# Moving averages in three parts at three places of a tile, and all of memory's weights loaded ahead of the first head

## The chip, the cores and the metric

The kernel runs on one core of a Trainium2 chip. The metric is the device time of one execution in microseconds (us). The core has five engines with an instruction stream each: TensorE (PE in the profile, its weight loads PEld), VectorE (DVE), ScalarE (ACT), GpSimd (POOL) and SyncE (SP), which here only issues DMA transfers. TensorE's results go to PSUM, of which one "bank" holds 128 x 512 numbers in f32.

## The reference

One layer of a hybrid encoder over 2048 rows of 1024 numbers: an attention with forget gates beside a pooling over moving averages, then a cross attention to 256 memory rows, then a SwiGLU network. What the change touches lies in the first projection, the pooling, and the memory's keys and values:

```python
xn = rmsnorm(h, g_mix)
z = einsum('bsd,dc->bsc', xn, w_in)        # q, k, v (512 each), p_in (512), f_logit (8)
q, k = rmsnorm(q heads, g_q_fox), rmsnorm(k heads, g_k_fox)
c = cumsum(log_sigmoid(f_logit))           # along the sequence
fox = softmax(q.k / 8 + c[t] - c[s], s <= t) . v
mixed_g = trailing mean of p_in over POOL_WINDOWS[g] - p_in     # windows 2, 4, 8, 16
pool = concat(mixed_g . w_pool[g]) * pool_scale
h = h + concat(fox, pool) . w_out
...
mkv = rmsnorm(mem, g_mem_kv) . w_mem_kv    # memory's keys and values
```

## The kernel before

**Products.** Operands of f32 are split in two: a rounded high part, which ACT writes as a cast (L199, or L194 where a gain is applied), and the rest, which VectorE writes as a subtraction (L55). A product is three matmuls (`mm3`, L60 to L62): high by high, high by low, low by high. The cast and the subtraction together are called a split; the second needs the first.

**Order.** From L236 to the end of the memory projection the order of PE, VectorE, ACT, POOL and SP is the order in which the code is written. An engine that stands at an instruction whose inputs are late holds up all that is written behind it on that engine.

**The tiles.** After a first part that makes the pooling's columns (p_in) and splits the weights, sixteen projection tiles i of 128 rows follow (15 in a loop, the last written out). A tile is four quarters n; a quarter (`project`) is 24 matmuls of 128 x 386 into one of four banks "z", which ACT empties with a scaling into z (`scaled`). Between the quarters of tile i the code puts:

- after quarters 0 and 1, `to_heads`: PE turns the heads of tile i-2 (transposes, L425) into three banks "tp", ACT copies them out and SP stores them. Their source kl is the split of the normed heads;
- then `po()`: ACT empties the pooling's one bank "ss" (L493) and POOL stores it; then `pooled`, the three matmuls of one average of the tile before into that bank;
- after quarter 2, `window`: the averages of this tile. VectorE scales and sums (L204, g+1 sums for window 2 << g), takes the mean minus the frame (L474), and then the average is split (ACT L199, VectorE L55) into two new slots "jl". Tiles 0, 3, 6 and 9 make two averages, tiles 1, 2, 4, 5, 7, 8, 10 and 11 one, the others none;
- after quarter 3, `split_heads` for tile i-1: two products on VectorE (L411, L413) norm the heads in cb, ACT casts them to kl (L416), VectorE subtracts (L55).

Fourteen slots jl of 128 x 528 are shared by averages, pooling results, weights on the way in and out (`out_sums`, stores of wo_t at L518), and the gates' cumulation; a freed slot is taken again in the order of freeing, and a taker waits for the slot's last readers, stores among them.

**The last tile** runs its quarters in the order 3, 2, 1, 0. Behind quarter 3 stand four small matmuls of the memory's mean squares (L660, into "ss", from a slot jl). `gates` adds a bias to the gates' logits (L384). `cumulated` is a generator whose phases are put between other work by `next(cum)`: POOL makes a triangle (L529); minimum and doubling on VectorE and exponential and logarithm on ACT (L534 to L537); a difference (L539); two products of PE into "ss" and a running total on POOL; the last sum (L549); a turn by PE, a copy (L553) and a store to memory, from which `load_gates` spreads it over 128 partitions (cb).

**The memory projection** follows: `kv(n)`, n = 0 to 15, six matmuls of 128 x 512 each, from weights that SP loads (`load_kv`, L566, raw in kr) and ACT and VectorE split (`split_kv`, L194 and L195, into kw). Six weights come early; the other ten are loaded here, eight ahead of the first head's loads and two behind kv(4), into eight buffers kr, eight buffers kw. `load_head` fetches the first head of the attention in parts n of 512 columns (qs, kh, kl). In the middle stand the norm's sums for the last tile (L394), its `split_heads` (behind kv(4)) and its transposes (behind kv(7)). The attention starts with a mask on POOL (L832, from cb) and its scores on PE (L841).

The loop's order in code, which the change rewrites:

```python
for n in range(4):
    zps.update(project(i, j, hs, ls, (n,)))
    if n < 2 and i > 1:
        to_heads(i - 2, zr, range(2 * n, 2 * n + 2))
    for po in pos:
        po()
    ...
    if n < 3:
        scaled(i, n, z, zps[n])
    if n == 2:
        nxt = [(w, window(...)) for w in averages(i)]
...
if i > 0:
    zr = split_heads(*st_)
```

Of the kernel before, what the change touches and what calls it, by code (L numbers as in the profile page):

```python
# [25 lines left out]
NG = 4  # L26
# [14 lines left out]
def block_kernel(ctx: ExitStack, tc: tile.TileContext, x, xT, memT, cols, rows, w_qkvf, w_p, w_pool, w_out,  # L41
# [194 lines left out]
    with xstack, in_order(EN.DVE, EN.Activation, EN.Pool, EN.SP):  # L236
# [171 lines left out]
        def split_heads(z, qn, rq):  # L408
# [5 lines left out]
                               op=ALU.mult)  # L414
            zr = slab(2, zs_home, F32R)[:].rearrange("p (h a d) -> p h a d", h=2 * H, a=2)
# [33 lines left out]
        def window(g, T, s):  # L449
# [29 lines left out]
            mh, ml = Slot(F32R), Slot(F32R)  # L479
            split(mh.v, ml.v, mixed)  # L480
# [81 lines left out]
        def load_kv(n):  # L562
            a, k = divmod(n, KD)
            s = Slot() if n < EARLY else None
            kvraw[n] = s, s.v if s else kvp.tile([P, MW], F32, tag="kr", name="kr", bufs=8)[:]
            sp.dma_start(kvraw[n][1], w_mem_kv[k * P:(k + 1) * P, a * MW:(a + 1) * MW])  # L566

        def split_kv(n):
# [5 lines left out]
            else:  # L574
                t_ = kvp.tile([P, 2, MW], F32R, tag="kw", name="kw", bufs=8)
# [22 lines left out]
        for b in range(NB):  # L598
            hs, ls = x_parts(xt)
            for j in range(2):  # L600
# [15 lines left out]
                for n in range(4):  # L616
                    zps.update(project(i, j, hs, ls, (n,)))
                    if n < 2 and i > 1:
                        to_heads(i - 2, zr, range(2 * n, 2 * n + 2))
                    for po in pos:  # L620
                        po()
                    pos = []
                    if mxs:
# [4 lines left out]
                    if n == 2:  # L628
                        nxt = [(w, window(w % NG, w // NG, pts.pop(w))) for w in averages(i)]
                mxs = nxt  # L630
                if i < 6:
                    square_rows(i + 10)
                if i > 0:
                    zr = split_heads(*st_)
# [18 lines left out]
        z, vq = slab(i % 2), slab(3)  # L653
        cum = cumulated()
        next(cum)
        zp3 = project(i, 1, hs, ls, (3,))[3]
        ssp = one_bank()
# [17 lines left out]
        scaled(i, 1, z, zp1)  # L675
# [4 lines left out]
        next(cum)  # L680
# [11 lines left out]
        next(cum)  # L692
        split_kv(4)
# [13 lines left out]
        for n in range(EARLY + 8, 2 * KD):  # L707
            load_kv(n)
# [1102 lines left out]
```

## Time and profile before

| | us |
|---|---|
| median of 3 runs | 2616.28 (2612.10 to 2616.97) |
| the profiled execution | 2612.79 |
| its span, first to last instruction | 2610.8 |
| ahead of the tiles, 0 to 102.2 | 102.2 (PE busy 95.1) |
| sixteen tiles, 102.2 to 437.4 | 335.2 |
| memory projection and start of attention, 437.4 to 515 | 77.6 |
| attention, cross attention, network, 515 to 2610.8 | 2095.8 (PE busy 2050.4) |

The durations in the trace come from the one profiled execution. Of the page, one reads first the busy time of each engine, then the chain of work that ended last (PE 47% of it; the next are "issue" with 8% and VectorE with 2%), then where PE is idle and what it waits for. A row of the trace gives start, duration, engine, line, operation, output<-inputs, tile and shape, and in brackets the idle time ahead of it with what ended it. TensorE's clock can be granted at less than full speed; a view by windows gives the mean grant for any stretch (1.00 is full).

### The profile page before, as it was taken

What the parts mean: (1) busy time and instruction counts of PE and PEld (TensorE: products, weight loads), DVE (VectorE), ACT (ScalarE), POOL (GpSimd) and SP (SyncE); (2) the same over time, 40 slices, a digit from 0 to 9 for tenths busy, and PEclk for the clock granted to TensorE, in tenths of its full rate; (3) what the DMA queues carried; (4) which work ended last, traced back from release to release, by engine and by line L of the source; (5) the groups of instructions that cost most, each with busy time, mean ns of one, the idle gap of its engine ahead of it and who ended that gap; (6) DMA issues with size and microseconds to landing.
All of it is one profiled execution on the core that took longest, in us unless ns stands there. A gap on an engine that the chain in (4) does not pass through costs nothing.

```text
span 2610.8 us, 37299 instructions
## 1 busy us (share of the span) xinstructions
PE 2524.1 (97%) x12909; PEld 2162.6 (83%) x12909; DVE 1730.0 (66%) x2998; ACT 1300.5 (50%) x2487; POOL 825.8 (32%) x1135
## 2 busy tenths in 40 slices
PE   8999898899999899999999999999999999999998
PEld 8989898688888677788878888888888888888887
DVE  4465654799999755454787788656766666664554
ACT  5544344688989622555643433334553333333443
POOL 0022333455545521444524454441001122222000
PEclk9999999999999999999999999999999999999999
DMA  8655565754542645322554554447773233334765
GB/s 278 206 158 157 156 194 176 232 145 124 140 129 62 193 145 180 131 81 94 176 211 154 191 180 174 173 162 244 260 256 139 93 125 105 115 107 165 242 208 187
DMA packets 246765, 434.00 MB, mean 166 GB/s; under 512 B 30000, under 2 KB 119856, under 8 KB 238896
## 3 DMA queue, kind: packets, MB, share of 16 engines
q1 hardware_dynamic: 213104, 322.54, 39.1%
q0 software_dynamic: 33472, 109.08, 11.6%
q8 instruction: 102, 1.67, 0.3%
q14 instruction: 87, 0.71, 0.1%
HBM read 294.02 MB, written 137.50 MB: 165 GB/s over the span
## 4 chain that ended last, share of the span: by engine, by line
PE 47%; issue 8%; DVE 2%; ACT 1%; DMA 1%; POOL 1%; SPq 0%; POOLq 0%; DVEq 0%; ACTq 0%
PE bk L60 13%; PE bk L62 13%; PE bk L61 13%; PE mmps L60 2%; PE mmps L62 2%; PE mmps L61 2%; PE tp L1022 1%; DMA xraw<-hTd 0%; DVE ww L55 0%; POOL out_dram L1704 0%; DMA h<-h1d 0%; ACT mq L1195 0%; DMA hTd<-hst 0%; DVE ms L1199 0%; ACT pm L1224 0%
## 5 line engine op out<-in xcount | busy, mean ns | idle before, releaser
L55 DVE TENSOR_TENSOR ww<-draw,ww 128x512 fp32r<-128x512 f32 x308 | 205.1, 702 | 156.5 <-ACT ww L199 156.0
L199 ACT CAST ww<-draw 128x512 fp32r<-128x512 f32 x308 | 179.6, 620 | 220.4 <-PE bk L62 173.3
L55 DVE TENSOR_TENSOR ww<-graw,ww 128x512 fp32r<-128x512 f32 x220 | 177.6, 814 | 106.5 <-ACT ww L199 106.2
L61 PE MATMUL bk<-ww,ww 128*128 128x512 f32 x616 | 239.6, 389 | 0.0
L60 PE MATMUL bk<-ww,ww 128*128 128x512 f32 x616 | 239.6, 389 | 0.0
L62 PE MATMUL bk<-ww,ww 128*128 128x512 f32 x616 | 239.6, 389 | 0.0
L199 ACT CAST ww<-graw 128x512 fp32r<-128x512 f32 x220 | 135.9, 622 | 181.2 <-PE bk L62 159.5
L55 DVE TENSOR_TENSOR pl<-tp,ph 128x512 fp32r<-128x512 f32 (+3 forms) x296 | 176.9, 599 | 32.4 <-ACT ph L935 30.5
L60 PE MATMUL zps<-wh,xhi 128*128 128x386 f32 x512 | 176.6, 345 | 0.0
L854 ACT ACTIVATE s<-s,mx 128x1024 f32<-128x1024 f32 (+2 forms) x192 | 173.7, 905 | 4.7 <-DVE mx L848 4.2
L62 PE MATMUL zps<-wh,xl 128*128 128x386 f32 x512 | 175.0, 342 | 0.0
L61 PE MATMUL zps<-wl,xhi 128*128 128x386 f32 x512 | 174.9, 342 | 0.0
L919 PE MATMUL tp<-ident,s 128*128 128x128 f32 x1088 | 171.8, 273 | 3.1 <-DVE pl L55 2.5
L935 ACT CAST ph<-tp 128x512 fp32r<-128x512 f32 (+3 forms) x296 | 148.8, 514 | 39.8 <-PE tp L919 34.0
L919 PEld LDWEIGHTS tp<-ident,s 128*128 128x128 f32 x1088 | 133.9, 141 | 31.6 <-DVE pl L55 6.7
L1704 POOL DMA_DIRECT2D out_dram<-o x32 | 17.3, 542 | 382.5 <-DVE o L1701 381.5
L62 PE MATMUL bk<-qs,ww 128*128 128x512 f32 x352 | 137.2, 390 | 1.1 <-DVE ww L55 1.1
L60 PE MATMUL bk<-qs,ww 128*128 128x512 f32 x352 | 137.8, 392 | 0.3 <-ACT s L1623 0.3
L61 PE MATMUL bk<-kh,ww 128*128 128x512 f32 x352 | 137.0, 389 | 0.0
L60 PE MATMUL bk<-kl,ww 128*128 128x512 f32 x352 | 136.9, 389 | 0.0
L61 PE MATMUL bk<-cb,ww 128*128 128x512 f32 x352 | 136.9, 389 | 0.0
L62 PE MATMUL bk<-kl,ww 128*128 128x512 f32 x352 | 136.9, 389 | 0.0
(612 smaller groups left out, 7276.8 us busy)
## 6 DMA issues: line engine op xcount, KB each, us to landing
graw<-in_w_gu_dram SPq DMA_DIRECT2D x44, 1024.0 KB, 5.4
draw<-in_w_down_dram SPq DMA_DIRECT2D x66, 256.0 KB, 4.5
xl<-in_xT_dram SPq DMA_DIRECT2D x64, 256.0 KB, 4.4
wdr<-in_w_down_dram SPq DMA_DIRECT2D x22, 512.0 KB, 4.6
jl<-in_x_dram SPq DMA_DIRECT2D x32, 256.0 KB, 6.9
vd<-cb SPq DMA_DIRECT2D x16, 512.0 KB, 3.7
cb<-cd SPq DMA_DIRECT2D x8, 1024.0 KB, 7.2
v<-vd SPq DMA_DIRECT2D x8, 1024.0 KB, 5.1
```

The source lines that it names most:

```text
L55: (eng or dve).tensor_tensor(out=lo, in0=src, in1=f(hi), op=ALU.subtract)
L60: pe.matmul(ps, lhsT=sh, rhs=mh, start=first, stop=False, skip_group_check=goes_on)
L61: pe.matmul(ps, lhsT=sh, rhs=ml, start=False, stop=False, skip_group_check=goes_on)
L62: pe.matmul(ps, lhsT=sl, rhs=mh, start=False, stop=last, skip_group_check=goes_on)
L199: act.copy(hi, raw)
L854: act.activation(s[:, sl], s[:, sl], AF.Exp, bias=ng, scale=-1.0, accum_out=l[:, q, g:g + 1])
L919: pe.transpose(tp[:, q * P:(q + 1) * P], unit["rows"][q][:, j * P:(j + 1) * P], ident[:])
L935: act.copy(ph[:, sl], tp[:, sl])
L1022: pe.transpose(tp[:, e_], src[:, q + e_], ident[:])
L1704: pool.dma_start(out[rows_, cs], o)
```

## The change

The tile loop: `split_heads` loses its two products to a new `norm_heads`; `window` ends with the mean, and its split becomes `window_cast` (ACT) and `window_rest` (VectorE). The averages' sums now stand behind quarter 0, their casts behind quarter 1, followed by the norm products of tile i-1 and the averages' subtractions; `split_heads` (cast and subtraction) comes right behind quarter 3. `po()` moves ahead of `to_heads`.

The last tile: the memory's mean squares move behind quarter 2, the heads' norms and split ahead of the cumulation's second phase, the cumulation's products behind quarter 1, its last sum behind kv(1).

The memory projection: ten buffers kr and seven kw; ten loads in one go; the gates' load between parts 1 and 2 of the first head; the last tile's transposes behind kv(8).

```diff
-        def split_heads(z, qn, rq):
+        def norm_heads(z, qn, rq):
             qf = qn.rearrange("p (h d) -> p h d", d=DH)
...
+        def split_heads(z, qn, rq):
+            qf = qn.rearrange("p (h d) -> p h d", d=DH)
             zr = slab(2, zs_home, F32R)[:].rearrange("p (h a d) -> p h a d", h=2 * H, a=2)
             act.copy(zr[:, :, 0, :], qf)
...
-            mh, ml = Slot(F32R), Slot(F32R)
-            split(mh.v, ml.v, mixed)
+            return s
+
+        def window_cast(s):
+            mh = Slot(F32R)
+            act.copy(mh.v, s.t[:, HIS:])
+            return s, mh
+
+        def window_rest(s, mh):
+            ml = Slot(F32R)
+            sub_hi(ml.v, s.t[:, HIS:], mh.v)
             s.free()
             return mh, ml
...
-            kvraw[n] = s, s.v if s else kvp.tile([P, MW], F32, tag="kr", name="kr", bufs=8)[:]
+            kvraw[n] = s, s.v if s else kvp.tile([P, MW], F32, tag="kr", name="kr", bufs=10)[:]
...
-                t_ = kvp.tile([P, 2, MW], F32R, tag="kw", name="kw", bufs=8)
+                t_ = kvp.tile([P, 2, MW], F32R, tag="kw", name="kw", bufs=7)
...
-                    if n < 2 and i > 1:
-                        to_heads(i - 2, zr, range(2 * n, 2 * n + 2))
                     for po in pos:
                         po()
                     pos = []
+                    if n < 2 and i > 1:
+                        to_heads(i - 2, zr, range(2 * n, 2 * n + 2))
...
-                    if n == 2:
-                        nxt = [(w, window(w % NG, w // NG, pts.pop(w))) for w in averages(i)]
+                    if n == 0:
+                        wins = [(w, window(w % NG, w // NG, pts.pop(w))) for w in averages(i)]
+                    if n == 1:
+                        wins = [(w, window_cast(s_)) for w, s_ in wins]
+                        if i > 0:
+                            norm_heads(*st_)
+                        nxt = [(w, window_rest(*s_)) for w, s_ in wins]
                 mxs = nxt
+                if i > 0:
+                    zr = split_heads(*st_)
                 if i < 6:
                     square_rows(i + 10)
-                if i > 0:
-                    zr = split_heads(*st_)
...
         zp3 = project(i, 1, hs, ls, (3,))[3]
+        scaled(i, 3, z, zp3)
+        gates(i, z)
+        norm_heads(*st_)
+        zr = split_heads(*st_)
+        next(cum)
+        zp2 = project(i, 1, hs, ls, (2,))[2]
         ssp = one_bank()
...
-        scaled(i, 3, z, zp3)
-        gates(i, z)
         next(cum)
-        zr = split_heads(*st_)
...
-        zp2 = project(i, 1, hs, ls, (2,))[2]
-        next(cum)
-        next(cum)
...
         zp1 = project(i, 1, hs, ls, (1,))[1]
+        next(cum)
...
         to_heads(i - 1, zr, range(4))
-        next(cum)
...
         kv(1)
         next(cum)
+        next(cum)
...
-        for n in range(EARLY, EARLY + 8):
+        for n in range(EARLY, 2 * KD):
             load_kv(n)
-        head0.extend(load_head(0, hpa, range(3)))
+        head0.extend(load_head(0, hpa, range(2)))
         load_gates(0, head0[3])
+        load_head_part(0, head0, 2)
...
         split_kv(7)
-        for n in range(EARLY + 8, 2 * KD):
-            load_kv(n)
+        norm_heads(*st_)
         zr = split_heads(*st_)
...
-        to_heads(LAST, zr, range(4), pool)
         split_kv(10)
         kv(8)
+        to_heads(LAST, zr, range(4), pool)
```

The order of instructions at three places. First VectorE in tile 3, from the mean of the first average to the split of the heads (jl are slots of averages, cb the normed heads, kl their split). Before:

```order
L474 SCALAR_TENSOR_TENSOR jl_1796<-jl_2129,jl_1796 128x512
L55 TENSOR_TENSOR jl_2133<-jl_1796,jl_2132 128x512
L204 TENSOR_TENSOR jl_1798<-jl_1798,jl_1794 128x512
L457 COPY jl_1798<-tail_1428 128x16
L459 COPY tail_1428<-jl_1798 128x16
L204 TENSOR_TENSOR jl_2139<-jl_1798 128x527
L204 TENSOR_TENSOR jl_2141<-jl_2139 128x525
L474 SCALAR_TENSOR_TENSOR jl_1798<-jl_2141,jl_1798 128x512
L55 TENSOR_TENSOR jl_2145<-jl_1798,jl_2144 128x512
L411 TENSOR_TENSOR cb<-qs,zrq 128x1024
L413 TENSOR_TENSOR cb<-cb,gqs 128x1024
L55 TENSOR_TENSOR kl<-cb,kl 128x16x64
```

and after, VectorE at the same place:

```order
L477 SCALAR_TENSOR_TENSOR jl_1796<-jl_2059,jl_1796 128x512
L204 TENSOR_TENSOR jl_1798<-jl_1798,jl_1794 128x512
L460 COPY jl_1798<-tail_1428 128x16
L462 COPY tail_1428<-jl_1798 128x16
L204 TENSOR_TENSOR jl_2065<-jl_1798 128x527
L204 TENSOR_TENSOR jl_2067<-jl_2065 128x525
L477 SCALAR_TENSOR_TENSOR jl_1798<-jl_2067,jl_1798 128x512
L411 TENSOR_TENSOR cb<-qs,zrq 128x1024
L413 TENSOR_TENSOR cb<-cb,gqs 128x1024
L55 TENSOR_TENSOR jl_2120<-jl_1796,jl_2114 128x512
L55 TENSOR_TENSOR jl_2122<-jl_1798,jl_2116 128x512
L55 TENSOR_TENSOR kl<-cb,kl 128x16x64
```

The two subtractions L55 of the averages, which stood each behind its own average, now stand together behind both averages and behind the two norm products.

Second, VectorE in the last tile, from the gates' bias (L384) to the turned sums (jl is here the slot of the cumulation, mms the memory's mean squares). Before:

```order
L384 TENSOR_TENSOR fl<-kh,rowt 128x8
L534 TENSOR_SCALAR jl_4432<-fl 128x128
L535 SCALAR_TENSOR_TENSOR jl_4432<-jl_4432,fl 128x128
L411 TENSOR_TENSOR cb<-qs,zrq 128x1024
L413 TENSOR_TENSOR cb<-cb,gqs 128x1024
L55 TENSOR_TENSOR kl<-cb,kl 128x16x64
L667 COPY mms<-ss 128x2
L539 TENSOR_TENSOR jl_4432<-jl_4432 128x128
L545 COPY jl_4432<-ss 128x128
```

and after, VectorE between the same two ends:

```order
L384 TENSOR_TENSOR fl<-kh,rowt 128x8
L411 TENSOR_TENSOR cb<-qs,zrq 128x1024
L413 TENSOR_TENSOR cb<-cb,gqs 128x1024
L55 TENSOR_TENSOR kl<-cb,kl 128x16x64
L545 TENSOR_SCALAR jl_4430<-fl 128x128
L546 SCALAR_TENSOR_TENSOR jl_4430<-jl_4430,fl 128x128
L550 TENSOR_TENSOR jl_4430<-jl_4430 128x128
L686 COPY mms<-ss 128x2
L55 TENSOR_TENSOR cb<-kh,cb 128x8x64
L556 COPY jl_4430<-ss 128x128
```

The heads' three instructions moved ahead of the gates' first two, and the split of the values (cb<-kh,cb) ahead of the copy of the cumulation's products from "ss".

Third, VectorE in the memory projection at the cumulation's last sum, which is L549 before and L560 after (kw are split weights, zms the sums of squares of the last tile's heads). Before:

```order
L195 SCALAR_TENSOR_TENSOR jl_4558<-jl_4024,colt,jl_4557 128x512
L195 SCALAR_TENSOR_TENSOR jl_4562<-jl_4026,colt,jl_4561 128x512
L549 TENSOR_TENSOR jl_4432<-ss,jl_4433 128x128
L195 SCALAR_TENSOR_TENSOR kw<-jl_4028,colt,kw 128x512
L195 SCALAR_TENSOR_TENSOR kw<-jl_4204,colt,kw 128x512
L394 TENSOR_REDUCE zms<-cb 128x16
L553 COPY jl_4432<-ss 128x128
```

and after, VectorE in the same stretch:

```order
L195 SCALAR_TENSOR_TENSOR jl_4558<-jl_4024,colt,jl_4557 128x512
L195 SCALAR_TENSOR_TENSOR jl_4562<-jl_4026,colt,jl_4561 128x512
L195 SCALAR_TENSOR_TENSOR kw<-jl_4028,colt,kw 128x512
L195 SCALAR_TENSOR_TENSOR kw<-jl_4204,colt,kw 128x512
L394 TENSOR_REDUCE zms<-cb 128x16
L560 TENSOR_TENSOR jl_4430<-ss,jl_4431 128x128
L564 COPY jl_4430<-ss 128x128
```

The last sum moved behind two weights' splits and the reduction, right ahead of the copy of its own turn.

More of the change, by code (lines that the diff above doesn't have):

```diff
@@ L652, in block_kernel @@
         i = LAST
-        z, vq = slab(i % 2), slab(3)
         cum = cumulated()
         next(cum)
+        z, vq = slab(i % 2), slab(3)
         zp3 = project(i, 1, hs, ls, (3,))[3]
+        scaled(i, 3, z, zp3)
[4 more added lines that the diff above has]
+        zp2 = project(i, 1, hs, ls, (2,))[2]
         ssp = one_bank()
```

## The prediction

> **What bounds the kernel now.** I read the page first, then the stages in windows, then the waits of TensorE in the stage that the change touches, and last the single waits in order of time.
>
> ```profile
> span 2610.8 us, 37299 instructions
> PE 2524.1 (97%) x12909; PEld 2162.6 (83%) x12909; DVE 1730.0 (66%) x2998; ACT 1300.5 (50%) x2487; POOL 825.8 (32%) x1135
> 102.20:437.40 335.20, 314.73 (x1825) 308.15 (x1824) 195.90 (x299) 152.46 (x267) 98.56 (x103) 0.97 0.56 164
> 437.40:515.00 77.60, 63.90 (x309) 46.87 (x308) 51.05 (x135) 49.42 (x97) 29.98 (x54) 0.96 0.78 230
> ```
>
> TensorE is busy 97% of the span, so only time in which it stands or runs at a lower granted clock can be won. The windows' columns are length, then busy time of PE, PEld, DVE, ACT and POOL, then granted clock, share of the DMA engines and GB/s. The sixteen projection tiles (102 to 437 us) leave PE 20.5 us idle at a clock of 0.97; the memory projection and the start of attention behind it leave 13.7 us at 0.96. VectorE is busy for 196 of 335 us there: it is late in places, not overloaded. The waits of PE from 102 to 515 us by group (sum, times, longest), the first and the last of the four long ones in the tiles, and those of the memory projection:
>
> ```profile
> PE tp L425 <- DVE kl L55: 15.3, 6, 3.1
> PE ss L60 <- ACT jl L493: 4.3, 3, 1.4
> 184.06 1.21 PE L425 MATMUL tp<-identr,kl 128*128 128x128 f32 x8 [2.93 <-DVE kl L55]
> 317.12 1.20 PE L425 MATMUL tp<-identr,kl 128*128 128x128 f32 x8 [2.85 <-DVE kl L55]
> 420.40 1.83 PE L660 MATMUL ss<-ones,jl 128*128 128x1 f32 x8 [3.44 <-POOL jl L529]
> 455.00 1.18 PE L425 MATMUL tp<-identr,kl 128*128 128x128 f32 x12 [2.73 <-DVE kl L55]
> 471.93 0.80 PE L60 MATMUL kv<-kw,xhi 128*128 128x512 f32 x1 [4.36 <-ACT kw L194]
> ```
>
> Six times the transposes wait for the split of the normed heads (kl); the wait before 455.00 is one of them, the other five lie in tiles 3, 4, 7, 9 and 10 and make 15.3 - 2.73 = 12.6 us. Three times, in tiles 4, 7 and 10, the second pooling matmul waits for ACT to empty its one bank: 4.3 us. Together 16.9 us. The last three rows belong to the last tile and the memory projection.
>
> **The clock behind a wait.** The granted clock is the last but two of each row.
>
> ```profile
> 184.10:187.50 3.40, 3.40 (x15) 3.11 (x16) 2.58 (x4) 3.01 (x5) 0.49 (x1) 0.51 0.37 101
> 317.20:320.60 3.40, 3.40 (x15) 3.11 (x16) 3.30 (x8) 2.97 (x5) 2.14 (x4) 0.51 0.38 121
> 455.10:458.50 3.40, 3.39 (x25) 2.90 (x26) 1.33 (x3) 2.95 (x6) 2.07 (x3) 1.00 1.05 210
> 419.60:426.50 6.90, 6.10 (x22) 6.13 (x23) 5.68 (x11) 3.07 (x5) 0.96 (x3) 0.51 0.14 40
> 470.80:477.70 6.90, 5.78 (x13) 4.23 (x14) 3.27 (x5) 3.28 (x5) 1.88 (x4) 0.51 1.05 253
> ```
>
> Behind the first and the last of the four long waits in the tiles follow 3.4 us at half clock; behind the waits of 3.44 and 4.36 us nearly seven; behind that of 2.73 us none. Four stretches cost at most 4 x 3.4 x 0.49 = 6.7 us; I take 6.0 (1.5 each), since short transposes fill part of them. The two long ones cost 0.49 x 6.1 = 3.0 and 0.49 x 5.8 = 2.8 us. [...]
>
> **The tiles.** VectorE's chain in tile 3, from the first moving average to the split heads:
>
> ```profile
> 167.56 1.10 DVE L204 TENSOR_TENSOR jl<-jl,jl 128x512 f32<-128x512 f32 x1
> 169.59 0.69 DVE L474 SCALAR_TENSOR_TENSOR jl<-jl,jl 128x512 f32<-128x512 f32 x1
> 173.79 0.69 DVE L55 TENSOR_TENSOR jl<-jl,jl 128x512 fp32r<-128x512 f32 x1 [3.50 <-ACT jl L199]
> 174.40 1.07 DVE L204 TENSOR_TENSOR jl<-jl,jl 128x512 f32<-128x512 f32 x1
> 177.15 0.69 DVE L474 SCALAR_TENSOR_TENSOR jl<-jl,jl 128x512 f32<-128x512 f32 x1
> 179.18 1.22 DVE L411 TENSOR_TENSOR cb<-qs,zrq 128x1024 f32<-128x1024 f32 x1
> 182.77 1.23 DVE L55 TENSOR_TENSOR kl<-cb,kl 128x1024 fp32r<-128x1024 f32 x1 [1.11 <-ACT kl L416]
> ```
>
> VectorE starts the averages at 167.56 with nothing else to do, yet stands 3.5 us for ACT's cast, which waits behind the third scaling. With the sums together, both are done 3.44 us (174.40 to 177.84) after 170.28, at 173.7; the two norm products take it to 176.2, the two subtractions to 177.5, ACT's head cast (about 1.1 us) lies beside these, and the split ends near 178.8 instead of 184.0. PE wants it at 181.13: the wait goes, with some 2 us to spare. Tiles 4, 7, 9 and 10 have the same order, and 1.4 us waits go because the bank's reading now stands ahead of the head copies on ACT. Nothing is added: the same instructions run. **A: 16.9 + 6.0 = 22.9 us.** What is late next is PE itself.
>
> In later tiles an average also waits for a store that still reads its slot:
>
> ```profile
> 286.06 0.69 DVE L204 TENSOR_TENSOR jl<-jl 128x513 f32<-128x513 f32 x1 [9.06 <-DMA poolT<-jl]
> 270.69 2.14 POOL L518 DMA_DIRECT2D wo_t<-jl  x4 [10.36 <-DVE jl L204]
> ```
>
> With the slots taken in another order, the first sum of that tile needs the first of the four wo_t stores issued at 270.69; their landing has a median of 2.3 us, so it waits little where the old one waited 9.06. I price this at nothing: PE has slack there. At worst it brings half of A back.
>
> **The last tile and the memory projection.** Moving the four sums of squares (L660) behind the next projection takes away 3.44 us and its 3.0 of clock; the data, ready at 420.4, precede their new place at 421. The weights that PE waits for at 471.93 were asked for last:
>
> ```profile
> 445.05 3.70 SPq L566 DMA_DIRECT2D kr<-in_w_mem_kv_dram  x8
> 463.42 0.85 SPq L566 DMA_DIRECT2D kr<-in_w_mem_kv_dram  x2
> 471.15 0.72 ACT L194 ACTIVATE kw<-kr,colt 128x512 fp32r<-128x512 f32 x1 [8.91 <-DMA kr<-in_w_mem_kv_dram]
> 470.40 1.11 POOL L832 TENSOR_SCALAR_AFFINE_SELECT cm<-cb 128x128 f32<-128x128 f32 x3 [4.33 <-DMA cb<-cd]
> 477.57 0.34 PE L841 MATMUL sps<-kh,qs 128*128 128x256 f32 x1
> 460.00:470.00 10.00, 6.93 (x31) 4.57 (x29) 4.55 (x7) 2.25 (x4) 3.31 (x4) 1.00 1.02 325
> ```
>
> In one go, the last two leave some 17 us earlier: 4.36 + 2.8 us go. The DMA engines are full (1.02), so two loads ahead push the first head's parts back by about 2 us, but the gates (cb) move ahead of the third part. They arrived at 470.40 and should now land near 467, and PE, at the first scores at 477.57 before, reaches them near 471, so this cover holds, barely. The transposes of 455.00 come one weight later (1.4 us), and with the chain ahead of them earlier by about as much their 2.73 us go. Removed: 3.44 + 3.0 + 4.36 + 2.8 + 2.73 = 16.3 us.
>
> The change also **adds two waits** of PE. The gates' cumulation now follows the split of the heads:
>
> ```profile
> 421.06 0.23 DVE L534 TENSOR_SCALAR jl<-fl 128x128 f32<-128x128 f32 x1
> 421.65 0.31 ACT L536 ACTIVATE jl<-jl 128x128 f32<-128x128 f32 x1 [2.02 <-DVE jl L535]
> 423.27 0.40 ACT L537 ACTIVATE jl<-jl,ones 128x128 f32<-128x128 f32 x1
> 421.53 1.22 DVE L411 TENSOR_TENSOR cb<-qs,zrq 128x1024 f32<-128x1024 f32 x1
> 425.12 1.22 DVE L55 TENSOR_TENSOR kl<-cb,kl 128x1024 fp32r<-128x1024 f32 x1 [1.11 <-ACT kl L416]
> 443.19 1.21 DVE L394 TENSOR_REDUCE zms<-cb 128x16 f32<-128x1024 f32 x1
> 428.75 0.42 PE L60 MATMUL zps<-wh,xhi 128*128 128x386 f32 x1
> 437.29 1.67 PE L425 MATMUL tp<-identr,kl 128*128 128x128 f32 x16
> ```
>
> From 421.06 run first the heads (421.53 to 426.34: 4.8 us), then minimum and doubling (0.6), then exponential to logarithm (421.65 to 423.67: 2.0) and a difference (0.3): ready at 428.8. PE does two quarters of a tile in 8.5 us (428.75 to 437.29); no longer held from 416.96 (420.40 less 3.44), it has two more quarters and the sums of squares behind it by about 426.4: a wait of 2.5 us (first). Its totals then go through POOL, and the last sum stands behind the reduction of row 443.19. That reduction ends 7.1 us after PE's transposes of row 437.29 start; these now start near 435.1, so the sum is there at 442.5, while PE, in order, has done two weights (1.4 us each, six matmuls apart) by 439.4: 3.1 us (second). The trace of before has neither; the ends are 0, if VectorE runs ahead, and twice 4.36 + 2.8 = 14.3 us, if both become like the longest wait here. With 1.5 us of clock each I take 2.5 + 3.1 + 3.0 = 8.6 us, nearest to the four like waits, and 0.9 us more for small waits of the weights that PE now catches up with. **B: 16.3 - 9.5 = 6.8 us.**
>
> Seven weight buffers instead of eight (kw) cost nothing: the weight that reuses the first is split after four others have been used.
>
> **Sum.** 22.9 + 6.8 = 29.7 us. The profiled execution took 2612.79 us (span 2610.8 and 2.0 around it), which gives 2583.1. The median of the three runs is 2616.28, 3.5 above it; on that footing I predict 2586.6 us.
>
> **Rivals.**
> - *Half of A stays*: the averages wait for stores in the late tiles (as at 286.06) now at the head of a tile, and norms and split stand behind them in VectorE's order. For: 9 us waits exist. Against: the slots' last stores are older. 2586.6 + 11.5 = 2598.
> - *B comes to nothing*: the loads land no sooner as the engines are full, the gates hold up the first scores. For: share 1.02. Against: the order of the loads. 2593.4.
> - *The two added waits don't come* because VectorE and ACT arrive earlier than I reckon: 2586.6 - 8.6 = 2578.
> - *No clock is won*: the 6.0 us stay, for PE cools at other places instead, and the added waits lose none: 2586.6 + 6.0 - 3.0 = 2589.6. Against: the rows of 184.10 and 317.20. [...]
> - *Nothing is won*: VectorE's split stays as late, for the sums of the next tile push it: within 5 us of before, 2613.
> - *Slower*: ACT's cast of the averages now stands in the second quarter of a tile, and behind it the copies of turned heads (three banks) and the scalings (four banks). If the sums are late by more than about 13 us (three quarters of a tile at 4.3 us), PE finds no bank. To end 5 us above before, some 35 us must be lost: 3 us in each of the twelve tiles that hold averages, so sums 16 us late in all of them. 2622. The longest wait of a sum is 9.2 us, against it.
>
> **How the numbers follow.** Forecast 0.47; half of A stays 0.12; B nothing 0.15; no added waits 0.13; no clock won 0.06; nothing won 0.04; slower 0.03. The range from 2576 to 2601 holds the first five with some 2 to 3 us for the spread of the runs (2612.1 to 2616.97), and both ends of the added waits (2578 to 2592.3). Faster by over 0.2% (5.2 us, about what a measurement of this kernel can tell from no change) 0.93; within it 0.04; slower 0.03.
>
> **What would show it.** In the profile after, PE should have no wait of over 1 us for kl in tiles 3 to 10, none for the bank, and the granted clock of the projection stage should rise from 0.97 to about 0.99. PE should wait for VectorE at the cumulation's first product and at its turn. ACT should not wait for kr at the end of the memory projection, and the first scores should start near 448 us, some 30 us earlier than 477.57. Wrong I am if the transposes still wait, if POOL's first select waits for cb beyond PE's arrival, or if what is won by the first scores is lost before the end.

## The result, and the profile after

The changed kernel takes 2581.15 us (median of 4 runs, 2578.56 to 2587.50) against 2614.86 us (4 runs, 2612.10 to 2616.97): 33.7 us less, a ratio of 0.9875 with a 95% interval of 0.9854 to 0.9896. The prediction was 2586.6 us, between 2576 and 2601.

The page of the changed kernel, its span and the busy times of the engines:

```profile
span 2576.9 us, 37301 instructions
PE 2510.7 (97%) x12909; PEld 2154.4 (84%) x12909; DVE 1734.8 (67%) x2998; ACT 1299.4 (50%) x2487; POOL 822.0 (32%) x1135
```

The same instructions run in 33.9 us less. PE's busy time is shorter too (2510.7 after 2524.1 us), although its matmuls are the same 12909: some of them no longer run at half clock (the mean granted clock of the tiles was 0.97 and is 1.00). The stages of the changed kernel in windows (length, busy time of PE, PEld, DVE, ACT, POOL, granted clock, share of the DMA engines, GB/s): the sixteen tiles, then the memory projection up to the first scores.

```profile
102.20:409.10 306.90, 304.25 (x1825) 300.53 (x1824) 195.85 (x298) 152.24 (x267) 93.81 (x96) 1.00 0.61 180
409.10:444.10 35.00, 29.62 (x139) 22.59 (x138) 18.71 (x26) 19.39 (x32) 12.58 (x21) 0.95 0.81 238
```

The tiles took 335.2 us with PE idle for 20.5 and a clock of 0.97. They now take 306.9 us with PE idle for 2.7 and a clock of 1.00; of the 2.7 us, 2.47 are one of the two waits that the change adds, at the end of this stretch. The tiles' problem is gone; what is left stands in the groups of PE's waits from 102 to 490 us (sum, times, longest), the first five:

```profile
PE sps L858 <- DVE mx L860: 6.0, 4, 4.2
PE ss L563 <- DVE jl L560: 2.8, 1, 2.8
PE ss L554 <- DVE mms L686: 2.5, 1, 2.5
PE kv L61 <- DVE kw L195: 1.3, 3, 0.8
PE kv L60 <- ACT kw L194: 1.3, 2, 0.9
```

No group for kl and none for ACT's reading of the pooling's bank is among them. The second and third are the two added waits at the cumulation. The first is at the start of the attention, and one wait of 4.2 us in it was not foreseen.

**Where the time went.** The same matmul can be found in both traces; the difference of its two times, each from its span's start, is the lead of the changed kernel there. It is 24.5 us at the start of the last tile, 33.5 at the first scores, 30.0 after the first 120 us of attention, and 33.9 at the end. So 24.5 us came from the tiles, 9.0 from the last tile and the memory projection, 3.5 were given back at the start of the attention, and 3.9 came behind it, where nothing was changed. The table of leads below shows that the last piece is spread between executions, and that a second execution of the same kernel gave back 1.1 us at the start of the attention and not 3.5.

**The tiles.** VectorE's waits from 102 to 440 us, two groups of the kernel before:

```profile
DVE jl L55 <- ACT jl L199: 44.8, 17, 8.7
...
DVE jl L204 <- DMA poolT<-jl: 14.7, 2, 9.1
```

and the group of the changed kernel that answers to the first:

```profile
DVE jl L55 <- ACT jl L486: 6.1, 5, 1.7
```

VectorE stood 44.8 us for the averages' casts and now stands 6.1; the 14.7 us for stores that still read a slot are gone. Its wait for the cast of the heads (kl) grew from 30.1 to 47.7 us instead, but PE waits for none of it: here the idle time of VectorE cost something only where it made PE late. Tile 3 in time, VectorE and PE of the changed kernel:

```profile
163.71 1.07 DVE L204 TENSOR_TENSOR jl<-jl,jl 128x512 f32<-128x512 f32 x1
...
169.71 1.22 DVE L411 TENSOR_TENSOR cb<-qs,zrq 128x1024 f32<-128x1024 f32 x1
...
173.40 1.23 DVE L55 TENSOR_TENSOR kl<-cb,kl 128x1024 fp32r<-128x1024 f32 x1
...
180.15 0.80 PE L428 MATMUL tp<-identr,kl 128*128 128x128 f32 x8
```

The split of the heads ends at 174.6 us (173.40 + 1.23), 5.5 us before PE turns them; it used to end at 184.0 us, 2.9 us after PE wanted it. The chain also starts earlier, at 163.71 instead of 167.56, since each tile hands less lateness to the next (with the parts at their old place, in the kernel "parts late" below, it starts at 162.30). In the kernel before, VectorE went from the last subtraction to the norm products at 179.18 without a pause, and ACT's cast of the heads waited for them:

```profile
181.70 1.04 ACT L416 CAST kl<-cb 128x1024 fp32r<-128x1024 f32 x1 [1.92 <-DVE cb L413]
```

So in this tile the later place of the norm products and of the heads' split in the code held nothing up; the averages' chain ahead of them did.

**From the last tile to the attention.** The changed kernel in order of time:

```profile
404.27 0.38 PE L554 MATMUL ss<-jl,ones 128*128 128x128 f32 x1 [2.47 <-DVE mms L686]
...
416.43 0.47 PE L563 MATMUL ss<-ident,jl 128*128 128x128 f32 x1 [2.84 <-DVE jl L560]
...
442.67 1.12 POOL L849 TENSOR_SCALAR_AFFINE_SELECT cm<-cb 128x128 f32<-128x128 f32 x3 [2.74 <-DMA cb<-cd]
...
444.07 0.28 PE L858 MATMUL sps<-kh,qs 128*128 128x256 f32 x1
...
458.12 0.69 DVE L860 CUSTOM_DVE_ANT_0 s<-sps,cb 128x512 f32<-128x512 f32 x1 [4.08 <-DMA mkvd<-mkv]
...
458.87 0.80 PE L858 MATMUL sps<-kh,qs 128*128 128x512 f32 x1 [4.18 <-DVE mx L860]
```

The gates (cb) land 1.4 us ahead of the first scores. Then VectorE stands 4.08 us until the projection's results (mkv) are stored: its score rows s take their memory. PE finds no free bank for scores and stands too. Before, no wait of this group was longer than 1.2 us:

```profile
PE sps L841 <- DVE mx L843: 3.0, 4, 1.2
```

### The profile page after: what moved, and what is told of

It is laid out like the page before. It is cut to its first block, busy times and chain, and to the rows that moved or that the text cites. A ratio compares the mean times of both kernels' runs of the same rounds, so it can differ in the third digit from the quotient of the medians.

```text
span 2576.9 us, 37301 instructions
## 1 busy us (share of the span) xinstructions
PE 2510.7 (97%) x12909; PEld 2154.4 (84%) x12909; DVE 1734.8 (67%) x2998; ACT 1299.4 (50%) x2487; POOL 822.0 (32%) x1135
## 3 DMA queue, kind: packets, MB, share of 16 engines
q8 instruction: 102, 1.67, 0.3%
## 4 chain that ended last, share of the span: by engine, by line
PE 49%; issue 8%; DVE 2%; ACT 1%; DMA 1%; POOL 1%; SPq 0%; POOLq 0%; DVEq 0%; ACTq 0%
PE bk L62 13%; PE bk L60 13%; PE bk L61 13%; PE mmps L60 2%; PE mmps L62 2%; PE mmps L61 2%; PE tp L1039 1%; DVE ww L55 0%; PE obk L60 0%; PE obk L61 0%; PE obk L62 0%; DMA xraw<-hTd 0%; POOL out_dram L1721 0%; DMA wqr<-in_w_mem_q_dram 0%; DMA h<-h1d 0%
## 5 line engine op out<-in xcount | busy, mean ns | idle before, releaser
L55 DVE TENSOR_TENSOR ww<-draw,ww 128x512 fp32r<-128x512 f32 x308 | 205.2, 702 | 155.6 <-ACT ww L199 155.1
L55 DVE TENSOR_TENSOR ww<-graw,ww 128x512 fp32r<-128x512 f32 x220 | 177.8, 815 | 105.9 <-ACT ww L199 105.5
L55 DVE TENSOR_TENSOR pl<-tp,ph 128x512 fp32r<-128x512 f32 (+3 forms) x296 | 176.7, 599 | 27.8 <-ACT ph L952 26.0
L60 PE MATMUL zps<-wh,xhi 128*128 128x386 f32 x512 | 174.6, 341 | 0.0
L952 ACT CAST ph<-tp 128x512 fp32r<-128x512 f32 (+3 forms) x296 | 148.7, 514 | 38.3 <-PE tp L936 32.8
```

The source lines that it names most:

```text
L55: (eng or dve).tensor_tensor(out=lo, in0=src, in1=f(hi), op=ALU.subtract)
L60: pe.matmul(ps, lhsT=sh, rhs=mh, start=first, stop=False, skip_group_check=goes_on)
L952: act.copy(ph[:, sl], tp[:, sl])
```

## The experiments

Each changes the kernel before or the changed kernel in one respect. The lead is that over the profile of the kernel before, at the same matmuls (102, 408, 477.6 and 600 us of before, and the end). At 102 us, where the tiles start, nothing has been changed yet: what stands there, up to 1.4 us, is spread between executions, and is taken off where the text speaks of a lead from the tiles' start.

| kernel | tiles' start | last tile | first scores | 600 us | end | median us |
|---|---|---|---|---|---|---|
| changed | -0.1 | 24.5 | 33.5 | 30.0 | 33.9 | 2581.15 |
| changed, again | 0.0 | 24.7 | 33.8 | 32.6 | 30.7 | 2582.93 |
| tiles alone | 0.7 | 25.4 | 24.6 | 23.8 | 19.6 | 2590.89 |
| memory alone | 1.4 | 0.9 | 9.7 | 7.3 | 6.3 | 2609.22 |
| loads 8 and 2 | 0.9 | 25.6 | 28.2 | 27.3 | 26.9 | 2587.01 |
| parts late | 0.9 | 25.5 | 33.0 | 29.8 | 29.3 | 2583.79 |
| one go early | 0.1 | 14.4 | 22.1 | 19.8 | 14.4 | 2594.36 |
| bank read late | 0.7 | 20.5 | 27.7 | 24.5 | 25.5 | 2586.54 |
| rows elsewhere | 1.0 | 25.6 | 33.3 | 28.4 | 26.8 | 2585.07 |
| cumulation early | 1.1 | 25.8 | 37.5 | 35.9 | 33.7 | 2578.53 |
| the same, again | 1.3 | 25.9 | 37.6 | 36.8 | 37.0 | 2578.71 |
| second head later | 0.3 | 24.9 | 32.7 | 30.2 | 29.8 | 2583.89 |
| later and early | 0.2 | 24.8 | 37.4 | 35.9 | 34.7 | 2579.97 |

From the tiles' start, the lead at the last tile is 24.6 or 24.7 us in all ten rows of the table that have the new tile loop whole or with its parts late. What the tile loop wins therefore repeats almost exactly.

### Each half alone

The first kernel takes the new tile loop into the kernel before, the second the new last tile and memory projection:

```diff
 # tiles alone: last tile as before
+        norm_heads(*st_)
         zr = split_heads(*st_)
...
 # memory alone: tile loop as before
                     if n == 2:
                         nxt = [(w, window(w % NG, w // NG, pts.pop(w))) for w in averages(i)]
```

> The kernel before with the change of the tile loop alone; last tile and memory projection stay as they were. Theory (the two halves add up): PE is 24.5 us earlier at the start of the last tile, as in the changed kernel, the waits of 3.44, 2.73 and 4.36 us behind it stay, and the time is 2614.9 - 24.5 = about 2590 us. Rival (the tiles' gain needs the memory loads, because PE then runs ahead of weights asked for late): the waits of the memory projection grow by 5 us or more and the time is 2595 us or above.

> The kernel before with the change of the last tile and the memory projection alone; the tile loop stays as it was. Theory: the five long waits for kl and the three for the bank stay, the first scores start about 9 us earlier than 477.57, about 3.5 us of it are given back at the start of the attention, and the time is about 2609 us (2606 to 2610). Rival (the memory part is worth nothing): 2613 to 2616 us.

2590.89 us (ratio 0.9910, 0.9889 to 0.9931) and 2609.22 us (0.9985, 0.9974 to 0.9997): both theories hold. PE's waits with the tiles alone, three groups:

```profile
PE kv L60 <- ACT kw L194: 6.4, 2, 5.7
...
PE ss L676 <- POOL jl L540: 3.4, 1, 3.4
PE tp L428 <- DVE kl L55: 2.8, 1, 2.8
```

The three waits behind the tiles stay, the one for the late weights 1.3 us longer. In the table the halves add up at the first scores, 24.6 + 9.7 = 34.3 against 33.5; from the tiles' start they are 23.9 + 8.3 = 32.2 against 33.7, so they add up to within 1.5 us. The memory part alone is worth 8 to 10 us at the first scores but only some 5 in the median.

### What in the tile does it

Three kernels undo one part each of the new tile loop. In the first all three parts stand behind the third quarter, where the averages were before; in the second each average is made in one go behind the first quarter; in the third the bank is read behind the transposes again:

```diff
 # parts late
-                    if n == 0:
+                    if n == 2:
                         wins = [(w, window(w % NG, w // NG, pts.pop(w))) for w in averages(i)]
-                    if n == 1:
+                    if n == 2:
                         wins = [(w, window_cast(s_)) for w, s_ in wins]
...
 # one go early
                     if n == 0:
-                        wins = [(w, window(w % NG, w // NG, pts.pop(w))) for w in averages(i)]
-                    if n == 1:
-                        wins = [(w, window_cast(s_)) for w, s_ in wins]
-                        if i > 0:
-                            norm_heads(*st_)
-                        nxt = [(w, window_rest(*s_)) for w, s_ in wins]
+                        nxt = [(w, window_rest(*window_cast(window(w % NG, w // NG, pts.pop(w))))) for w in averages(i)]
+                    if n == 1 and i > 0:
+                        norm_heads(*st_)
 # bank read late
-                    for po in pos:
-                        po()
-                    pos = []
                     if n < 2 and i > 1:
                         to_heads(i - 2, zr, range(2 * n, 2 * n + 2))
+                    for po in pos:
+                        po()
+                    pos = []
```

> The changed kernel with all three parts and the norm products behind the third quarter, where the averages stood before. Theory A (sums of both averages ahead of their casts are enough): the split of the heads ends about 2 us before PE wants it, no wait for kl over 1 us in tiles 3 to 10, 2581 us. Theory B (the earlier place is what matters): waits for kl of 1 to 3 us come back in tiles 3, 4, 7, 9 and 10 and the time is 2588 us or above.

> The changed kernel, but each average is made in one go (sums, cast, subtraction) behind the first quarter. Theory A (the earlier place is enough): no wait for kl over 1 us in tiles 3 to 10, PE at the start of the last tile within 1 us of the changed kernel, 2581 us. Theory B (the three parts are what matters): the waits come back at least in tiles 3 and 9, which make two averages, 2 to 3 us each with 1.7 us of half clock, 2586 us or above.

> The changed kernel with the bank's reading behind the transposes and their copies again. Theory: the three waits for the bank in tiles 4, 7 and 10 come back, 1.4 us each, no half clock behind them, and PE is 4.3 us later at the start of the last tile; 2585 us. Rival (ACT was late because of the averages' casts, which now stand elsewhere): waits under 0.5 us, 2581 us.

**Parts late:** a lead of 25.5 us at the last tile (24.6 from the tiles' start), 2583.79 us, and no group for kl: theory A. The sums of both averages ahead of their casts, with the norm products between casts and subtractions, are enough; the early place is not needed. VectorE still stands 21.4 us for the averages' casts and 18.2 us for stores that read a slot, up to 8.0 us at a time, and PE loses nothing by it.

**One go early:** theory A was right about kl, for which PE no longer waits, and wrong about the time, 2594.36 us. So the early place alone takes these waits away as well, if with less to spare: in tile 3 the split of the heads ends 2.8 us before PE turns them, not 5.5. Another wait came in tile 1. The kernel with one go early, ACT and PE:

```profile
133.90 0.62 ACT L486 CAST jl<-jl 128x512 fp32r<-128x512 f32 x1 [6.43 <-DVE jl L480]
134.43 0.68 ACT L504 ACTIVATE jl<-ss,colt 128x512 f32<-128x512 f32 x1
...
135.16 0.80 PE L60 MATMUL ss<-jl,jl 128*128 128x512 f32 x1 [6.68 <-ACT jl L504]
```

ACT stands 6.43 us at the cast of sums that VectorE has not made yet; behind it on ACT stands the reading of the pooling's bank, for which PE waits. With 1.4 us more at 253 us and 6.8 us of half clock that begin within the long wait, the lead falls from 24.5 to 14.4 us. That is close to the mechanism of the prediction's slower rival (a cast of late sums holds up the emptying of banks on ACT), in one tile instead of twelve. So the cast may stand apart from its sums (changed kernel) or both late (parts late), but not with them in the first quarter.

**Bank read late:** the three waits come back, 1.42 us each, with no half clock behind them: the theory. From the tiles' start the lead at the last tile is 4.9 us smaller (19.8 against 24.7); PE loses 1.62 us at each of the three, 0.20 more than the wait itself. So the new order of the bank's reading is worth its 4.3 us and a little more by itself. One of the three on PE, and on ACT ahead of it the two copies of turned heads and then the bank:

```profile
185.41 1.07 ACT L430 COPY st<-tp 128x512 f32<-128x512 f32 x2 [4.06 <-PE tp L428]
186.37 0.70 ACT L504 ACTIVATE jl<-ss,colt 128x512 f32<-128x512 f32 x1
```

```profile
187.13 0.49 PE L60 MATMUL ss<-jl,jl 128*128 128x512 f32 x1 [1.42 <-ACT jl L504]
```

### The memory's loads and the cumulation

The first kernel asks for two of the ten weights late again; the second moves the gates' phases back ahead of the heads' norms, and the last sum ahead of the third weight's split:

```diff
 # loads 8 and 2
-        for n in range(EARLY, 2 * KD):
+        for n in range(EARLY, EARLY + 8):
             load_kv(n)
...
         split_kv(7)
+        for n in range(EARLY + 8, 2 * KD):
+            load_kv(n)
 # cumulation early
         gates(i, z)
-        norm_heads(*st_)
-        zr = split_heads(*st_)
         next(cum)
...
+        norm_heads(*st_)
         next(cum)
         dve.tensor_copy(mms[:], ssp[:, :2])
         rsqrt(mr[:], mms[:])
+        zr = split_heads(*st_)
...
         to_heads(i - 1, zr, range(4))
+        next(cum)
...
         kv(1)
         next(cum)
-        next(cum)
```

> The changed kernel, but two of the ten weights are again asked for behind the fourth projected weight. Theory (the order of asking counts): PE waits about 4.4 us for the fifteenth weight with up to 2.8 us of half clock, the first scores start 4 to 7 us later than 444.1, and the time is 2584 to 2588 us. Rival (the DMA engines are full, so only their sum counts): no wait over 1.5 us there, 2581 us.

> The changed kernel with the gates' second phase ahead of the heads' norms again, and the last sum ahead of the third weight's split. Theory: the waits of 2.47 and 2.84 us at the cumulation's first product and turn go, with 1.7 us of half clock behind the second; the first scores start about 437 us and the time is about 2574 us. Rival (the full DMA engines set the start of the attention): the first scores are earlier, but the wait of 4.18 us near 458.9 grows by as much, and the time stays at 2580 to 2582 us.

**Loads 8 and 2:** 2587.01 us, as the theory said, with a wait of 2.81 us instead of its 4.4. The kernel with two late loads, ACT and PE:

```profile
444.00 0.72 ACT L194 ACTIVATE kw<-kr,colt 128x512 fp32r<-128x512 f32 x1 [7.43 <-DMA kr<-in_w_mem_kv_dram]
...
444.77 0.79 PE L60 MATMUL kv<-kw,xhi 128*128 128x512 f32 x1 [2.81 <-ACT kw L194]
```

The order of asking counts, though the DMA engines are full (share 0.98 to 1.03 from 424 to 444 us of the changed kernel); the first scores are 5.3 us later than in the changed kernel (28.2 against 33.5). From the tiles' start it is 6.4 us, some 1.5 of which come from 3.41 us of half clock behind the first added wait, which the changed kernel did not have there. What is left of it at 600 us can't be told: 2.7 us against one execution of the changed kernel, 5.3 against the other.

**Cumulation early:** both waits are gone, but 2578.53 us is neither the theory's 2574 nor the rival's 2580 to 2582. From the tiles' start the lead at the first scores is 36.4 us against 33.7, so 2.7 us larger and not 7. PE now catches up with the weights; its waits, the first three groups:

```profile
PE sps L858 <- DVE mx L860: 3.6, 4, 1.8
PE kv L60 <- ACT kw L194: 3.3, 3, 2.0
PE kv L61 <- DVE kw L195: 1.9, 5, 0.8
```

The weights' waits grew from 1.3 + 1.3 to 3.3 + 1.9 us, which takes 2.6 us of the 7. Behind the longest, of 2.0 us, PE is busy for 3.41 us at half clock from 423.9 us, which takes 1.7 more and leaves 2.7. So what was won is partly lost again, as the rival would have it, but at the weights, not at the start of the attention: the long wait there became smaller (1.8 us).

### The start of the attention

The first kernel gives the score rows s2 other memory; the second asks for the second head's data one unit later; the third does that together with the early cumulation:

```diff
 # rows elsewhere
         tpool.tile([P, 96], F32, name="pad")
+        for n in (0, 1, 3):
+            spool.tile([P, 512 * (n + 1)], F32, tag=f"s{n}", name=f"s{n}", bufs=4)
 # second head later
-                if b == (1 if h else 2) and h + 1 < H:
+                if b == (1 if h else 3) and h + 1 < H:
                     heads[h + 1] = load_head(h + 1, (hpa, hpb)[(h + 1) % 2])
```

> The changed kernel; the attention's 1536-column score rows (s2) take memory that the memory projection's results (mkv) did not use, by setting aside the buffers s0, s1 and s3 ahead of s2. Theory (the wait of 4.18 us near 458.9 is VectorE waiting until mkv is stored, since s2 takes its memory): the wait goes, with the 6.8 us of half clock behind it, PE is 5 to 7 us earlier at 480 us, and the time is 2574 to 2577 us. Rival (the full DMA engines deliver something else just as late, the next head's parts or the values): another wait of 3 us or more follows before 480 us, and the time is 2580 us or above.

> The changed kernel with the loads of the second head (3 MB and its gates) asked for one unit of scores later, behind the first head's third unit. Theory (the DMA engines are full from about 424 to 470 us, and what the first head waits for shares them with the second head's loads): the stores of mkv and the normalizers' way through memory land several us earlier, the wait of 4.18 us near 458.9 falls below 1.5 us with no half clock behind it, no wait of 3 us follows before 500 us, and the time is 2575 to 2578 us. Rival (only the sum of the bytes counts): the first head's waits go, but the second head's first scores, at 485.2 us now, wait for its parts or gates by 4 us or more, and the time is 2581 us or above.

> The same later loads of the second head together with the gates' cumulation early (as in the run of that name). Theory: the two gains add up, PE is 8 to 11 us ahead of the changed kernel at 500 us, and the time is 2570 to 2574 us. Rival: PE arrives still earlier at the second head's first scores and waits there for what it has won; 2577 us or above.

**Rows elsewhere:** the wait goes (no wait of this group is over 0.9 us), so shared memory was its cause. The time does not fall (2585.07 us): the rival. The kernel with the rows elsewhere, POOL and PE:

```profile
476.23 1.51 POOL L906 TENSOR_TENSOR fo<-fo,lbs 64x512 f32<-64x512 f32 x1 [6.31 <-DMA lbs<-ld]
...
478.62 0.22 POOL L943 MEMSET ph<- 128x128 f32 x1
...
478.90 0.58 PE L923 MATMUL acc<-ph,v 128*128 128x256 f32 x1 [5.96 <-POOL ph L943]
```

POOL stands 6.31 us for the first normalizers, which go through memory (ld, lbs); behind that stands the clearing of ph, for which PE waits 5.96 us. A wait on one late transfer gave way to a longer one on the next: from the tiles' start, the lead at 505 us of before is 34.4 us, against 30.0 and 31.9 in the two executions of the changed kernel, and at 515 us, behind that wait, it is 27.4.

**Second head later:** neither theory. The wait near 458.6 is still 3.03 us, against 4.18 and 2.90 in the changed kernel's two executions, and PE has a new wait of 1.1 us for POOL; the lead at 600 us is 30.2 us, as in the changed kernel (30.0 and 32.6). The second head's loads are not what delays the stores. The wait, and the stretch from 455 to 460 us of the same kernel (the last but one is the share of the DMA engines):

```profile
458.56 0.50 PE L858 MATMUL sps<-kh,qs 128*128 128x512 f32 x1 [3.03 <-DVE mx L860]
...
455.00:460.00 5.00, 1.97 (x9) 1.30 (x8) 2.20 (x8) 1.58 (x3) 1.06 (x4) 0.96 0.06 18
```

The DMA engines are nearly idle there (0.06; 1.07 in the changed kernel), and yet VectorE stands for the stores until 457.80. So full engines are not the whole reason for this wait. The first head's last part and its values are asked for at the same time as these stores and may delay them; that was not tried and stays open.

**Later and early:** 2579.97 us and a lead of 35.9 us at 600 us, no more than the early cumulation alone (35.9 and 36.8). Here the long wait did shrink, to 1.10 us, and at 505 us of before the lead from the tiles' start is 38.3 us, against 35.0 and 34.8 with the early cumulation alone. Two new waits of PE for POOL, 1.07 us before 485.37 and 1.91 us before 511.54, take these 3 us back. So neither gain was lost at the second head's first scores, where the rival had put it, but nothing of the sum is left.

### The spread

> The changed kernel once more, for the spread of one program. Theory (what differs between executions behind the attention is where the half-clock stretches fall): the profile repeats the waits of 2.47, 2.84 and 4.18 us up to 480 us within 1.5 us, the stretch from the first product with w_out to the end is between 1721 and 1726 us with other half-clock stretches, and the median is 2579 to 2584 us. Rival (the first profile is typical to the end): half-clock stretches at the same places and 2579 us.

> The early cumulation once more, beside the changed kernel on the same chip. Theory: 4 to 6 us of the 7 us that its two waits and their clock took are kept to the end of the attention, and its median is 2.5 to 5 us under that of the changed kernel. Rival (all of it is given back behind the attention): the medians agree within 1 us.

**Changed, again:** the theory. Up to the first scores the traces agree within 0.3 us; the wait for the stores is 2.90 instead of 4.18 us, and 3.41 us of half clock follow it instead of 6.83. With both, the second execution is 2.4 us ahead at 600 us, from the tiles' start. The wait:

```profile
457.31 0.79 PE L858 MATMUL sps<-kh,qs 128*128 128x512 f32 x1 [2.90 <-DVE mx L860]
```

From the first product with w_out to the last matmul it took 1724.0 us (1721.5 the first time, 1723.0 in the profile of before), with half-clock stretches at 839 and 891 us that the first profile lacks. From 600 us to the end it lost 2.0 us of its lead where the first profile won 3.9; over the thirteen traces of the table this piece lies between -5.4 and +3.9 us. So those 3.9 us are spread and no effect of the change.

**The same, again:** the median is 4.2 us under that of the changed kernel on the same chip, the theory. Over 8 runs each, the medians are 2581.7 us (changed; 2578.6 to 2587.5) and 2578.5 us (cumulation early; 2575.1 to 2583.0). In the two pairs of traces the early cumulation is ahead by 5.8 and 4.2 us at 600 us, by 4.6 and 2.9 from the tiles' start. The 3.2 us between the medians are likely but not certain: the ranges overlap, and of the 64 pairs of one run each the early cumulation is the faster in 54.

## Why the prediction came out as it did

- **Term A, 22.9 us: right, 24.5 measured** (24.7 from the tiles' start, with the tiles alone too; 23.2 between their medians). The step on VectorE's chain was right in kind: the sums ahead of the casts remove the wait, as "parts late" shows, though the early place alone would have done it too. Its spare time was put at 2 us and is 5.5, because the chain starts 3.9 us earlier; the sum had moved it from the old start. That the store of a slot would hardly be waited for also held, and in "parts late", where it is waited for, it costs PE nothing. All four half-clock stretches in the tiles went. The 1.8 us on top fit the 0.20 us that PE lost beside each wait in "bank read late": eight waits would make 1.6 us, an estimate.
- **Term B, 6.8 us: 9.0 at the first scores; at 600 us 5.5 in the first execution and 8.0 in the second.** The added waits were priced at 2.5 and 3.1 us and are 2.47 and 2.84. The mis-sized term was the clock behind them: 3.0 us were taken, and the first wait cost none in this trace, the second 1.6 (3.2 us of work at half). The same first wait did cost a stretch of 3.41 us in four other kernels (loads 8 and 2, parts late, rows elsewhere, second head later), so here it was luck. 16.3 removed, less 2.5 + 2.8 + 1.6 + 0.9, gives 8.5 of the 9.0.
- **What was left out:** that the attention's start gives back 3.5 us, in the second execution 1.1. The prediction reckoned up to the first scores and took the lead as kept to the end, though it named the loss of it as what would make it wrong. PE came 33.5 us earlier, the stores of mkv did not keep up with it, and where the longest wait had been 1.2 us there was one of 4.18 us, or 2.90, with half clock behind it.
- **The rival "B comes to nothing"** was half right: waits for transfers do return part of B, but behind the first scores, not before them. That the engines are full there (share 1.07 from 455 to 460 us of the changed kernel) is only part of the reason, as "second head later" shows with a share of 0.06 and a wait of 3.03 us; the rest is open.
- **The total.** Against its own execution 2583.1 us was forecast, and the profiled one took 2578.56 us. Of these 4.5 us, 1.6 are A, 2.2 are B up to the first scores, 3.5 go the other way at the start of the attention, and 3.9 came behind it by the spread; the other 0.3 lies around the span. Of the 5.5 us to the median, 1.4 are the footing: with a fourth run the median of before is 2614.86 us, not 2616.28. The forecast was right in its mechanism; that it came this close owes something to errors that offset each other and to where the half clock fell.

## What to carry to other kernels

Where an engine's order is fixed, as here, look for a chain "sum, cast on another engine, subtraction" that is made per item: made so, it cost VectorE 44.8 us in 17 waits for the casts, and 6.1 us in 5 with all sums first, then all casts, then all subtractions. Put between them work that waits for nothing. Starting the chain earlier can do as well, where its end then comes in time. Count only the stalls that reach the engine that bounds the time: here 47.7 us of VectorE's waits for the cast of the heads cost nothing. What was won ahead of a stage that waits for transfers was partly given back there (3.5 us and 1.1 us in two executions): follow the lead matmul by matmul, past the stage that was changed. And look at what an instruction queues behind itself before moving it earlier: the same cast that gained nothing by being early cost 10 us by standing ahead of a bank's reading.

## What the runs showed of the hardware

In the traces of the kernel before and of the changed kernel the half-clock stretches begin whole multiples of 3.4133 us apart, within 0.003 us, and last 3.413 or 6.827 us, but for one at the end of each trace. The rows that follow are windows of that grid; the last but two is the granted clock. The kernel before, at tile 3's wait of 2.93 us and at the 2.73 us wait before 455.00:

```profile
180.73:184.14 3.41, 0.48 (x4) 0.16 (x3) 2.16 (x2) 1.59 (x3) 0.00 (x0) 1.00 0.00 0
184.14:187.55 3.41, 3.41 (x15) 3.12 (x16) 2.63 (x4) 2.97 (x5) 0.54 (x1) 0.50 0.38 104
...
450.38:453.79 3.41, 1.89 (x9) 1.20 (x7) 2.21 (x3) 1.24 (x2) 0.00 (x0) 1.00 0.99 344
453.79:457.20 3.41, 2.19 (x19) 1.99 (x20) 2.39 (x3) 2.70 (x6) 0.77 (x1) 1.00 1.05 213
457.20:460.61 3.41, 3.41 (x17) 2.72 (x15) 0.75 (x1) 3.41 (x7) 2.33 (x4) 1.00 1.02 282
```

The first wait lies in one window, in which PE is idle for 2.93 us, and the next window has a clock of 0.50. The second is shared by two windows (PE idle for 1.5 and 1.2 us), and the clock is 1.00 in both and in the next. The changed kernel has a longer wait of 3.04 us, before 888.75, which lies across two windows (1.6 and 1.5 us idle); the clock is 1.00 there and behind it:

```profile
883.87:887.28 3.41, 1.84 (x9) 1.18 (x7) 2.76 (x3) 1.24 (x2) 2.71 (x3) 1.00 0.21 77
887.28:890.69 3.41, 1.94 (x8) 1.61 (x9) 2.01 (x4) 0.00 (x0) 0.00 (x0) 1.00 0.72 230
890.69:894.10 3.41, 3.41 (x17) 2.82 (x16) 1.19 (x2) 0.90 (x2) 0.56 (x1) 1.00 1.04 290
```

In windows of this grid, behind the first 7 us of these two traces, PE was idle for 2.28 to 3.40 us in each of the 16 full-clock windows that half clock followed, and for 1.77 us at most in those that full clock followed. In the five half-clock windows that another followed it was idle for 0.73 to 1.67 us, in those that full clock followed for 0.33 us at most. The waits of 2.73 and 3.04 us above went with no half clock, that of 2.93 us with one window of it, and those of 3.44 and 4.36 us (before) and 4.18 us (changed) with two; two windows at half clock cost an estimated 3.4 us (2 x 3.41 x 0.5). That is one source of the spread of the runs: behind the same wait at the start of the attention, 4.18 us in one execution of the changed kernel and 2.90 us in the other, stood 6.83 and 3.41 us of half clock.
